# Reordering the early loads and bias adds of a 4096-cubed matmul with bias and tanh on one Trainium2 core

## Chip, cores and metric

One NeuronCore of one Trainium2 chip runs the kernel. The metric is the device time of one execution in microseconds (us); the span in a profile, from the first to the last instruction, is about 1.7 us shorter.

## The reference

```python
m, k, n = 4096, 4096, 4096          # a, b, bias: random normal float32
return np.tanh(np.matmul(a, b) + bias)
```

## The kernel before

The matmuls are fp16 with float32 sums in PSUM: 32 row tiles of A, 32 k-tiles, output columns in 4 blocks of 1024 (two matmuls of 512 columns each). For columns 0 to 1023 the first eight row tiles run as two groups of four, g0 and g1, a few k-tiles at a time, so that matmuls can start while A and B are still arriving. Half-finished sums are set aside in SBUF ("spill"), and fills are matmuls on zeros. The steady loop comes after that and is not touched by the change. All loads that cast to fp16 are issued by GpSimd, in one queue; the kernel has at most eight of them in flight, each new issue waiting for the landing eight places before it.

The opening, cut (the comments are mine):

```python
fill(WARM, NB)                          # 11 matmuls on zeros
for t, copy in enumerate((nc.scalar.copy, nc.vector.tensor_copy)):
    load_b_low(nc.sync, raw_b[:, ds(t, 1), :], 0, t, 1)     # float32, 512 KB
    copy(b_cur[0][:, t, :], raw_b[:, t, :])                 # rounded to fp16
...
for m in g0:
    load_nat(m)                         # A's row tiles, 256 KB read each, GpSimd
...                                     # identity matrix
load_b_next(); load_b_next()            # B's third and fourth k-tile, GpSimd
turn_nat(0, nc.vector.tensor_copy); fill(3, P)   # 4 transposes on TensorE, one copy
turn_nat(1, nc.scalar.copy);        row(0, 0, 2)
turn_nat(2, nc.vector.tensor_copy); row(1, 0, 2)
turn_nat(3, nc.scalar.copy);        row(2, 0, 2); row(3, 0, 2)
```

The later loads and the end of the first eight row tiles, cut:

```python
want_a("g0c", G, 0, G * Q, KS, KM - KS)          # A, k-tiles 8 to 15, row tiles of g0
for u in range(KS, KM, 2):
    want(lambda u=u: load_b_all(u, 2))           # B, k-tiles 8 to 15
...
want(lambda: load_bias(bias_bc, 0, nc.gpsimd))
for t in (KM, KM + 8): ...                       # A for g1 and B, k-tiles 16 to 31
...
for t in (KM, KM + 8):
    for i in range(G):
        turn(ats[G + i], ("g1", t), i * Q, t, 8)        # VectorE transposes
    for m in g1 if t == KM else g0:
        for j in range(J):
            add_bias(m, j)                              # VectorE
    across(ps, g1, t, min(t + 8, KT - TB), KS)          # TensorE
turn(ats[0], ("g0", 0), 0, KM, KT - KM)                 # the first long transpose
down(ps, g1, KT - TB, KT, end)                          # g1 finished: add, tanh, store
...
for m in g0:
    for j in range(J):
        ...                                             # 16 matmuls
        if m < G - 1 and j == 0:
            turn(ats[m + 1], ("g0", m + 1), 0, KM, KT - KM)   # m = 0: the second one
        end(ps, m, j)
```

## Time and profile before

| | before |
|---|---|
| time, median of 3 runs | 1781.81 us (1781.77 to 1782.02) |
| span of the profiled run | 1780.2 us |
| TensorE busy | 1774.4 us, 100% |
| first real matmul | 7.44 us |
| breaks in TensorE's work after that | 0.08 us at 28.7, 0.21 at 35.8, 0.24 at 77.5 |

The page lists engine shares and the chain that ended last; the timeline prints start, duration, engine, source line, operation, what is written from what, the count, and in brackets the idle time before it and what ended it. PE is TensorE's matmuls, PEld its weight loads, DVE VectorE, ACT ScalarE, POOL GpSimd; L138 is line 138 of kernel.py, the matmul helper. On VectorE, L100 is a transpose of A, L176 and L149 add a PSUM bank to a spilled sum (L149 the last time), L181 adds the bias. A landing, below, is a load's issue plus its time to landing.

### The profile page before, as it was taken

Reading aid. Unit: us, or ns where it says so; the run is one execution under the profiler, and the core shown is the slowest. Engines: PE = TensorE matmul, PEld = TensorE weight load, DVE = VectorE, ACT = ScalarE, POOL = GpSimd, SP = SyncE. Lnnn points to the kernel's source line nnn. Section 1 sums busy time; section 2 is a strip of 40 time slices with the busy share of each in tenths; the row PEclk is TensorE's granted clock in tenths of the full one; section 3 lists DMA queues with packets and bytes.
Section 4 is the critical chain, followed back from the end, with each engine's and each line's share of the span. In section 5 each row is a group of like instructions: output and inputs, shape, how many; then the busy total and the mean of one; then the engine's idle time right before and its main releaser. Section 6 shows DMA issues by size and latency. Waiting matters only on the chain.

```text
span 1780.2 us, 20854 instructions
## 1 busy us (share of the span) xinstructions
PE 1774.4 (100%) x8254; PEld 806.9 (45%) x8254; DVE 763.8 (43%) x680; ACT 173.2 (10%) x279; POOL 872.1 (49%) x1618
## 2 busy tenths in 40 slices
PE   9999999999999999999999999999999999999999
PEld 4444444444444444444444444444444444444444
DVE  3764353444344443444344443444344443444342
ACT  2011000000000000000000000000000000000001
POOL 7465566544466554444456554444544454444510
PEclk9999999999999999999999999999999999999999
DMA  9999999976999877767699987766776667766641
GB/s 186 203 189 178 168 166 169 140 124 109 165 165 173 148 115 115 119 114 121 113 177 165 170 137 115 119 115 109 129 117 120 107 114 115 120 114 109 116 77 42
DMA packets 281393, 238.94 MB, mean 134 GB/s; under 512 B 159056, under 2 KB 231760, under 8 KB 281296
## 3 DMA queue, kind: packets, MB, share of 16 engines
q0 software_dynamic: 243280, 167.88, 70.1%
q1 hardware_dynamic: 37728, 69.62, 11.0%
q8 instruction: 64, 1.05, 0.2%
q14 instruction: 33, 0.27, 0.0%
q10 hardware_dynamic: 288, 0.13, 0.0%
HBM read 337.64 MB, written 67.11 MB: 227 GB/s over the span
## 4 chain that ended last, share of the span: by engine, by line
PE 99%; DMA 0%; issue 0%; ACT 0%; POOL 0%; DVE 0%; DVEq 0%; POOLq 0%
PE ps L412 93%; PE ps L138 6%; DMA nat<-in_a_dram 0%; ACT o_sb L152 0%; PE tp L257 0%; POOL nat L246 0%; DVE o_sb L149 0%; DVEq L149 0%; POOLq L435 0%
## 5 line engine op out<-in xcount | busy, mean ns | idle before, releaser
L412 PE MATMUL ps<-b,at 128*128 128x512 f16 x7712 | 1657.8, 378 | 0.0
L90 POOL DMA_DIRECT2D an<-in_a_dram x1492 | 805.5, 547 | 796.6 <-DVE at L100 583.4
L412 PEld LDWEIGHTS <-at 128*128 128x128 f16 x7712 | 754.6, 98 | 903.3
L100 DVE STREAM_TRANSPOSE at<-an 128x512 f16<-128x512 f16 (+1 forms) x380 | 565.6, 1539 | 85.8 <-DMA an<-in_a_dram 85.8
L149 DVE TENSOR_TENSOR o_sb<-ps,bias_bc 128x512 f32<-128x512 f32 (+1 forms) x243 | 165.4, 683 | 897.7 <-PE ps L412 695.7
L152 ACT ACTIVATE o_sb<-o_sb 128x512 f32<-128x512 f32 (+1 forms) x243 | 151.8, 626 | 1499.1 <-DVE o_sb L149 1499.1
L73 POOL DMA_DIRECT2D b<-in_b_dram x104 | 56.2, 544 | 15.5 <-DMA an<-in_a_dram 8.4
L138 PE MATMUL ps<-b,atx 128*128 128x512 f16 x256 | 56.2, 379 | 0.0
L138 PE MATMUL ps<-b,at 128*128 128x512 f16 x256 | 55.7, 379 | 0.1
L138 PEld LDWEIGHTS <-at 128*128 128x128 f16 x256 | 25.0, 98 | 30.5 <-DVE spill L181 0.5
L138 PEld LDWEIGHTS <-atx 128*128 128x128 f16 x256 | 24.6, 98 | 30.1 <-DVE atx L100 0.9
L100 DVE STREAM_TRANSPOSE atx<-an 128x512 f16<-128x512 f16 (+2 forms) x12 | 16.3, 1399 | 13.0 <-DMA an<-in_a_dram 13.0
L69 POOL DMA_DIRECT2D b<-in_b_dram x12 | 7.8, 654 | 22.4 <-PE ps L412 22.3
L152 ACT ACTIVATE spill<-spill 128x512 f32<-128x512 f32 x16 | 9.9, 632 | 85.6 <-DVE spill L149 85.5
L149 DVE TENSOR_TENSOR spill<-ps,spill 128x512 f32<-128x512 f32 x16 | 10.4, 678 | 9.9 <-PE ps L138 9.9
L181 DVE TENSOR_TENSOR spill<-spill,bias_bc 128x512 f32<-128x512 f32 x16 | 9.7, 680 | 0.0
L173 ACT COPY spill<-ps 128x512 f32<-128x512 f32 x16 | 8.0, 623 | 12.9 <-PE ps L138 12.9
L228 PE MATMUL ps<-zeros 128*128 128x512 f16 (+1 forms) x14 | 4.7, 498 | 1.3 <-DVE zeros L221 1.3
L176 DVE TENSOR_TENSOR spill<-ps,spill 128x512 f32<-128x512 f32 x8 | 4.8, 670 | 0.0
L228 PEld LDWEIGHTS <-zeros 128*128 128x128 f16 x14 | 1.6, 130 | 3.7 <-issue 2.4
L239 DVE CAST b<-spill 128x1024 f16<-128x1024 f32 x1 | 0.8, 849 | 4.5 <-DMA spill<-in_b_dram 4.5
L246 POOL DMA_DIRECT2D nat<-in_a_dram x4 | 2.3, 587 | 0.8 <-POOLq L435 0.8
(14 smaller groups left out, 8.9 us busy)
## 6 DMA issues: line engine op xcount, KB each, us to landing
an<-in_a_dram POOLq DMA_DIRECT2D x480, 192.0 KB, 5.1
out_dram<-o_sb SPq DMA_DIRECT2D x239, 256.0 KB, 2.7
an<-in_a_dram POOLq DMA_DIRECT2D x960, 32.0 KB, 2.7
b<-in_b_dram POOLq DMA_DIRECT2D x94, 256.0 KB, 8.2
b<-in_b_dram POOLq DMA_DIRECT2D x6, 1024.0 KB, 13.5
an<-in_a_dram POOLq DMA_DIRECT2D x32, 128.0 KB, 5.6
out_dram<-spill SPq DMA_DIRECT2D x16, 256.0 KB, 5.9
an<-in_a_dram POOLq DMA_DIRECT2D x12, 256.0 KB, 8.2
```

The costliest lines, as they stand in the source:

```text
L69: queue.dma_start(out=dst, in_=src[:, ds(t0 % BL, nt), :])
L73: nc.gpsimd.dma_start(out=bt[t0 // TB][ds(q * QP, QP), ds(t0 % TB, nt), :], in_=src.rearrange("(t p) n -> p t n", p=QP),)
L90: nc.gpsimd.dma_start(out=an[ds(q * QP, QP), :, ds((t - t0) * QP, n * QP)], in_=src.rearrange("(mb p) k -> p mb k", p=QP),)
L100: nc.vector.transpose(at[:, ds(t, n), :].rearrange("P t (mb p) -> P mb t p", p=QP), an[:, ds(mb0, Q), ds((t - t0) * QP, n * QP)].rearrange ...
L138: nc.tensor.matmul(ps, at[:, t, :], bt[t // TB][:, t % TB, ts(j, NB)], start=start, stop=stop)
L149: nc.vector.tensor_tensor(out=o_sb[:, piece], in0=ps[:, piece], in1=addend[:, piece], op=mybir.AluOpType.add)
L152: nc.scalar.activation(o_sb[:, piece], o_sb[:, piece], mybir.ActivationFunctionType.Tanh)
L173: nc.scalar.copy(aside(m, j), ps)
L176: nc.vector.tensor_tensor(out=aside(m, j), in0=ps, in1=aside(m, j), op=mybir.AluOpType.add)
L181: nc.vector.tensor_tensor(out=aside(m, j), in0=aside(m, j), in1=bias_bc[:, ts(j, NB)], op=mybir.AluOpType.add)
L228: nc.tensor.matmul(ps[:, ds(0, w)], zeros[:, :P], zeros[:, :w], start=i == 0, stop=i == n - 1)
L412: nc.tensor.matmul(ps, at[:, t, :], b_cur[t // TB][:, t % TB, ds(c0, w)], start=t == 0, stop=t == KT - 1,)
```

## The change

Its intent: the first matmul should not wait for two float32 k-tiles of B on SyncE's queue. Only the first stays there, rounded by two engines at once. The second goes to GpSimd's queue behind two row tiles. Later loads are split so that what is needed first lands first, and the bias moves back.

```diff
-    WARM = 11
+    WARM = 9
...
-    for t, copy in enumerate((nc.scalar.copy, nc.vector.tensor_copy)):
-        load_b_low(nc.sync, raw_b[:, ds(t, 1), :], 0, t, 1)
-        copy(b_cur[0][:, t, :], raw_b[:, t, :])
+    load_b_low(nc.sync, raw_b[:, ds(0, 1), :], 0, 0, 1)
+    for j, copy in enumerate((nc.scalar.copy, nc.vector.tensor_copy)):
+        copy(b_cur[0][:, 0, ts(j, NB)], raw_b[:, 0, ts(j, NB)])
...
-        copy(ats[m][:, ds(0, BL), :], tp)
+        for t in range(0, BL, 2):
+            copy(ats[m][:, ds(t, 2), :], tp[:, ds(t, 2), :])
...
-    for m in g0:
-        load_nat(m)
+    load_nat(0)
+    load_nat(1)
+    load_b_next()
+    load_nat(2)
     ...                                  # identity matrix
+    load_nat(3)
...
-    want_a("g0c", G, 0, G * Q, KS, KM - KS)
-    for u in range(KS, KM, 2):
-        want(lambda u=u: load_b_all(u, 2))
+    for t in (KS, KS + 4):
+        want_a(("g0", t), G, 0, G * Q, t, 4)
+        for u in (t, t + 2):
+            want(lambda u=u: load_b_all(u, 2))
...
-        for u in range(t, t + 8, TB):
-            want(lambda u=u: load_b_all(u, TB))
+        for u in (t, t + 2):
+            want(lambda u=u: load_b_all(u, 2))
+        if t > KM:
+            want(lambda: load_bias(bias_bc, 0, nc.gpsimd))
+        want(lambda t=t: load_b_all(t + TB, TB))
...
-        for m in g1 if t == KM else g0:
-            for j in range(J):
-                add_bias(m, j)
         across(ps, g1, t, min(t + 8, KT - TB), KS)
+    for m in g1:
+        for j in range(J):
+            add_bias(m, j)
     turn(ats[0], ("g0", 0), 0, KM, KT - KM)
     down(ps, g1, KT - TB, KT, end)
+    for m in g0:
+        for j in range(J):
+            add_bias(m, j)
```

Left out: the matmul order of the first two row tiles (one k-tile each, then fills, then the second k-tile), VectorE's transposes of A's k-tiles 8 to 15, cut in halves like their loads, and a later bias row loaded in two pieces.

More of the change, by code (lines that the diff above doesn't have):

```diff
@@ L257, in turn_nat @@
             nc.tensor.transpose(tp[:, t, :], nats[m][:, :, t], ident)
-        copy(ats[m][:, ds(0, BL), :], tp)
-    nats, b_done = {}, [2]
-    for m in g0:
-        load_nat(m)
+        for t in range(0, BL, 2):
+            copy(ats[m][:, ds(t, 2), :], tp[:, ds(t, 2), :])
+    nats, b_done = {}, [1]
+    load_nat(0)
+    load_nat(1)
+    load_b_next()
+    load_nat(2)
     nc.gpsimd.affine_select(
@@ L279 @@
     turn_nat(1, nc.scalar.copy)
-    row(0, 0, 2)
+    row(0, 0, 1)
+    row(1, 0, 1)
+    fill(4, P)
+    row(0, 1, 1)
     turn_nat(2, nc.vector.tensor_copy)
-    row(1, 0, 2)
+    row(1, 1, 1)
+    fill(3, P)
     turn_nat(3, nc.scalar.copy)
@@ L300 @@
     bias_bc = biasp.tile([P, NCW], fp32, name="bias_bc")
-    want(lambda: load_bias(bias_bc, 0, nc.gpsimd))
     for t in (KM, KM + 8):
         want_a(("g1", t), G, 4 * P, G * Q, t, 8)
-        for u in range(t, t + 8, TB):
-            want(lambda u=u: load_b_all(u, TB))
+        for u in (t, t + 2):
[3 more added lines that the diff above has]
+        want(lambda t=t: load_b_all(t + TB, TB))
     for m in g0:
@@ L325 @@
     ps = {}
-    for m in g0:
-        turn(ats[m], "g0c", m * Q, KS, KM - KS)
+    for t in (KS, KS + 4):
+        for m in g0:
+            turn(ats[m], ("g0", t), m * Q, t, 4)
     one_by_one(ps, g0, BL, KS, BL)
@@ L343 @@
             turn(ats[G + i], ("g1", t), i * Q, t, 8)
-        for m in g1 if t == KM else g0:
-            for j in range(J):
-                add_bias(m, j)
         across(ps, g1, t, min(t + 8, KT - TB), KS)
+    for m in g1:
+        for j in range(J):
+            add_bias(m, j)
     turn(ats[0], ("g0", 0), 0, KM, KT - KM)
     down(ps, g1, KT - TB, KT, end)
+    for m in g0:
+        for j in range(J):
+            add_bias(m, j)
     ahead = 3
@@ L398 @@
             bias_next = biasp.tile([P, NCW], fp32, name="bias_bc")
-            load_bias(bias_next, (c + 1) * NCW, nc.sync)
+            for h in range(2 if c == 0 else 1):
+                w = NCW // (2 if c == 0 else 1)
+                load_bias(bias_next[:, ds(h * w, w)], (c + 1) * NCW + h * w, nc.sync)
         pump()
```

## The prediction

> **What bounds the kernel now.** I read the engine shares first, then the chain that ended last, then the first 120 us in order of time, because the diff touches only work issued there.
>
> The page's engine rows and its chain of work:
>
> ```profile
> span 1780.2 us, 20854 instructions
> PE 1774.4 (100%) x8254; PEld 806.9 (45%) x8254; DVE 763.8 (43%) x680; ACT 173.2 (10%) x279; POOL 872.1 (49%) x1618
> PE 99%; DMA 0%; issue 0%; ACT 0%; POOL 0%; DVE 0%; DVEq 0%; POOLq 0%
> ```
>
> TensorE sets the time. The merged chain in order of time shows what little is not matmul:
>
> ```profile
> 1.31 0.68 POOL nat L246
> 2.00 5.12 DMA nat<-in_a_dram
> ...
> 9.79 25.99 PE ps L138 x120
> 35.78 0.05 issue
> 35.82 41.60 PE ps L138 x192
> 77.42 0.08 issue
> 77.50 41.60 PE ps L138 x192
> 119.10 1654.20 PE ps L412 x7680
> ```
>
> 41.60/192 = 0.217 us a matmul in the opening, 1654.20/7680 = 0.215 later. A saving can only come from the lead-in (7.4 us to the first real matmul) and from three small breaks. Two stand here: 35.82 starts 0.21 us and 77.50 about 0.24 us beyond the usual step. A third, 0.08 us, is at 28.70, below. Against 1781.8 us, 2% is 35.6 us: out of reach both ways unless something goes badly wrong.
>
> The timeline of the opening, TensorE, VectorE and the loads:
>
> ```profile
> 1.26 4.33 PE L228 MATMUL ps<-zeros 128*128 128x512 f16 x11 [1.26 <-DVE zeros L221]
> ...
> 5.88 0.85 DVE L239 CAST b<-spill 128x1024 f16<-128x1024 f32 x1 [4.53 <-DMA spill<-in_b_dram]
> ...
> 6.51 0.41 PE L257 MATMUL tp<-ident,nat 128*128 128x128 f16 x4 [0.91 <-DMA nat<-in_a_dram]
> ...
> 7.44 1.04 PE L138 MATMUL ps<-b,atx 128*128 128x512 f16 x4
> ...
> 27.93 2.50 DVE L100 STREAM_TRANSPOSE atx<-an 128x512 f16<-128x512 f16 x4 [6.30 <-DMA an<-in_a_dram]
> ...
> 28.69 6.59 PEld L138 LDWEIGHTS <-atx 128*128 128x128 f16 x32 [0.41 <-DVE atx L100]
> ```
>
> The reader should see that from 6.5 us TensorE never rests, and that at 28.69 it waits for VectorE, which waited for a load of A that landed at 27.85 (issued 19.34, 8.5 us to landing). That load has no slack.
>
> VectorE where the first pass ends, and a bias pass it did earlier:
>
> ```profile
> 76.36 4.86 DVE L181 TENSOR_TENSOR spill<-spill,bias_bc 128x512 f32<-128x512 f32 x8
> 85.07 2.31 DVE L100 STREAM_TRANSPOSE atx<-an 128x2048 f16<-128x2048 f16 x1 [3.85 <-DMA an<-in_a_dram]
> 87.31 4.90 DVE L149 TENSOR_TENSOR spill<-ps,spill 128x512 f32<-128x512 f32 x8
> 92.12 2.30 DVE L100 STREAM_TRANSPOSE atx<-an 128x2048 f16<-128x2048 f16 x1
> ```
>
> From 85.07 to 94.42 VectorE is full; its second long transpose feeds the row tile that TensorE reaches at 91.31 + 32 x 0.217 = 98.24. Slack: 3.8 us.
>
> **What the Trainium skill says.** "DMA: Bandwidth & Descriptors", section "Issuing engines are not separate DMA queues": loads issued by any engine run on the same 16 DMA engines and interleave, so issuing elsewhere saves sequencer time, not bandwidth. The trace agrees: the opening reads about 400 KB of float32 per us, whether from SyncE's queue (409 GB/s in 4 to 5 us) or from GpSimd's, whose page rate of about 200 GB/s counts the halved written bytes. "TensorE: Matmul & The Clock Gate", section "Part 1: The HAM clock gate": the clock is released after some 3.4 us of activity, not after a number of matmuls. The trace agrees: fills step by 0.427 us from 1.26 to about 4.9, then go twice as fast. The same page, section "Architectural detail", says VectorE's queue is strictly first in, first out. At 87.31 above it agrees: finished sums wait behind the 85.07 transpose, which waits for its load.
>
> **The change, part by part.**
>
> Lead-in. Before, both of B's first k-tiles (512 KB each, SyncE) precede A's row tiles (256 KB each read). Landings, issue plus time to landing: B0 4.6, B1 5.9, row tiles 6.5, 7.1, 7.8, 8.4, then B2 9.7, B3 10.9. That is 0.65 us per 256 KB. Now GpSimd's queue holds row 0, row 1, B1, row 2, row 3, B2, B3; the bytes are the same. Placing each landing by the KB before it: row 0 after 768 KB, two steps earlier, 5.2; row 1 5.8; B1 7.1; row 2, row 3, B2, B3 unchanged. Eleven fills less two at 0.427 cold, the last two already fast, end near 5.1, about when row 0 lands.
> B0 rounded in halves by ScalarE and VectorE costs some 0.5 us instead of ScalarE's 1.05, ready by about 5.2. First real matmul: row 0 lands at 5.2; before, landing to matmul took 7.44 - 6.46 = 1.0 us; so about 6.1, 1.3 us earlier. But row 2 lands at 7.8 and row 3 at 8.4 still. Row 3's four transposes then start near 8.65 (9.19 before), row 2's matmuls near 8.9 (9.6 before). So the lead is 0.7 us once all four rows run. The added fills, 7 x 0.06 = 0.4 us, mostly lie in waits for B1 and row 3.
>
> The lead then dies. TensorE would reach the 28.70 point at about 28.0, but its data land at 27.85 because loads up to there have the same order and bytes, and the DMA engines are busy. Ready at 28.64 as before. Worth: 0, or the 0.08.
>
> A's k-tiles 8 to 15 in two halves with B's between. B8 and B9, which ended the wait at 35.8 (landing 35.73: 28.13 + 7.6), now come after 4 small A loads instead of 4 large. Small ones land about 0.73 us apart, large ones 1.33. So 27.85 + 4 x 0.73 + 4 x 0.64 = 33.3, needed at 35.6: 0.21 us saved. Price: 8 x 0.73 - 4 x 1.33 = about 0.4 us more queue time for all later loads.
>
> B24 and B25 as two k-tiles with bias later: about 73.4 instead of 77.3, and 24 through 27 by 76.0, so the 0.24 us at 77.50 goes too. Together 0.45 us saved; TensorE ends the first group's last stage at about 90.9.
>
> Bias adds moved. Two passes of eight adds, 4.86 us each, ran at 61.05 and 76.36, when VectorE was otherwise waiting for loads. The first now runs at about 77.8 to 82.6, still free. The second now stands behind the last finished sums and ahead of the second long transpose, and there is no slack for it. Chain from the load that frees 85.07:
> - first long transpose: 85.07 to 87.31 (next start)
> - eight finished sums, spaced 0.6: to 92.1
> - eight bias adds, spaced 0.6: to 96.9
> - second long transpose, 2.30: to 99.2.
>
> TensorE wanted it at 98.24 before, at 97.8 now. So it waits some 1.4 us and restarts 0.95 us later than before; with the 0.4 us that the load behind the first transpose lost, 1.35 us later. After that VectorE catches up (5 us of work per 6.9 us row tile). The next A row's buffer is released 5 us later, but it landed at 109.4 for a transpose at 112.8, so I expect no second wait. From 119 to the end all is matmul and shifts as a block. The bias row in two pieces later costs nothing visible.
>
> Sum: lead-in 0, breaks -0.45, new wait about +1.8 = **+1.35 us: 1781.8 + 1.3 = 1783.1 us**.
>
> **The rivals.**
> First, the change works as intended: the loads of A for 28.70 come 0.7 us or more sooner because two queues fill the DMA ramp at 2 to 4 us better. For it: only 193 GB/s flow in 2 to 3 us, and in 16 to 18 us the rate sags below what such packets reach elsewhere, so there is room. Against it: the loads between wait for earlier landings (GpSimd has eight in flight), and B3, whose landing releases them, moves only if the total does. If the DMA stream gains 1 us throughout, the late chain starts 1 us earlier too: about 1782.0. If it gains 2 us, 1781.2.
> Second, GpSimd's first load may have a start-up of its own. Its first packet appears at 4.85 us, 3.5 us after issue, where later isolated issues take about 1.25. I read this as waiting behind SyncE's megabyte. If it is start-up instead, the DMA engines idle from about 3.9 to 4.8 and everything slips up to 0.9 us: 1784.0.
> Third, the bias adds slip into gaps: no wait at 98, total 1781.4. VectorE's order in the program speaks against it: the eight adds precede the transpose.
>
> **Range and chances.** All terms together move the time by under 3 us. I take **1783.1 us**, 8 in 10 within **1781.2 to 1784.3**. Chances: **faster by over 2% 0.003, within 2% 0.994, slower by over 2% 0.003**.
>
> **What would show it.** In the changed profile: first real matmul near 6.1; TensorE's loads at about 28.7 still waiting for VectorE, with a break near 0.7 us; no break at 35.8 or 77.5; L181-type adds at about 92 to 97 and, right behind, a weight load near 99 that waited over 1 us for the long transpose. The prediction is wrong if that weight load does not wait, or if the 28.7 break is absent because the loads came earlier, or if a new break appears before 20 us.

## More of the kernel before

In the records each load raises its semaphore in 16 steps, which I read as one per DMA engine. I call the time from first to last step the load's *spread*; it is worked out from the trace's semaphore records.

## The result and the profile after

| | before | after |
|---|---|---|
| time, median | 1781.91 us (4 runs, 1781.77 to 1782.03) | 1785.53 us (4 runs, 1784.90 to 1786.65) |
| ratio of the fast runs | | 1.0021, 95% interval 1.0004 to 1.0038 |
| span of the profiled run | 1780.2 us | 1784.9 us |

A ratio is the mean time of one kernel's fast runs over that of the other's in the same rounds, so it is not quite the ratio of the medians. The changed kernel is slower by 0.2%, inside the 2% band, but 3.6 us by the medians where I had 1.3, and outside my range. The profiled run is the slowest of its four; a second profile follows below.

The page's engine row and chain row after the change:

```profile
span 1784.9 us, 20891 instructions
PE 1774.9 (99%) x8259; PEld 805.9 (45%) x8259; DVE 763.7 (43%) x686; ACT 172.5 (10%) x281; POOL 876.2 (49%) x1631
PE 94%; DMA 3%; POOL 1%; issue 1%; DVE 1%; ACT 0%; DVEq 0%; POOLq 0%
```

TensorE's busy time is the same to 0.5 us, so what was added is waiting. The chain now leaves TensorE for 6% of the span: it runs through loads and VectorE up to 102.84 us and is pure matmul from there on.

The timeline of the opening after the change, TensorE alone:

```profile
5.20 0.41 PE L257 MATMUL tp<-ident,nat 128*128 128x128 f16 x4 [0.28 <-DMA nat<-in_a_dram]
...
6.80 0.41 PE L257 MATMUL tp<-ident,nat 128*128 128x128 f16 x4 [1.03 <-DMA nat<-in_a_dram]
...
7.05 1.23 PE L138 MATMUL ps<-b,atx 128*128 128x512 f16 x4
```

The first row tile arrives as early as intended: its transposes start at 5.20 instead of 6.51. The second is 1 us late, and TensorE idles for it.

Waits of TensorE from 20 to 54 us, after the change, from its timeline:

```profile
23.16 7.12 PE L138 MATMUL ps<-b,at 128*128 128x512 f16 x32 [0.54 <-DMA b<-in_b_dram]
30.78 20.89 PE L138 MATMUL ps<-b,atx 128*128 128x512 f16 x96 [0.50 <-DVE atx L100]
52.63 1.67 PE L138 MATMUL ps<-b,at 128*128 128x512 f16 x7 [0.95 <-DVE spill L176]
```

Two are for late loads, directly or through VectorE's transposes of them. The third waits for VectorE to empty a PSUM bank; VectorE had stood behind transposes whose load was late (49.51, before 46.08). The bracket subtracts part of the pipelined matmul; by start-to-start times less the usual 0.217 the three cost 0.71, 0.67 and 1.12 us. The breaks at 35.8 and 77.5 are gone.

VectorE after the change, around the end of group g1, and the weight load that waits for it:

```profile
81.75 4.91 DVE L181 TENSOR_TENSOR spill<-spill,bias_bc 128x512 f32<-128x512 f32 x8 [3.16 <-DMA bias_bc<-in_bias_dram]
88.67 2.31 DVE L100 STREAM_TRANSPOSE atx<-an 128x2048 f16<-128x2048 f16 x1 [2.02 <-DMA an<-in_a_dram]
90.91 4.84 DVE L149 TENSOR_TENSOR spill<-ps,spill 128x512 f32<-128x512 f32 x8
95.67 4.89 DVE L181 TENSOR_TENSOR spill<-spill,bias_bc 128x512 f32<-128x512 f32 x8
100.47 2.31 DVE L100 STREAM_TRANSPOSE atx<-an 128x2048 f16<-128x2048 f16 x1
```

```profile
102.83 1.19 PEld L138 LDWEIGHTS <-atx 128*128 128x128 f16 x7 [2.19 <-DVE atx L100]
```

This is the chain I had drawn: transpose, eight finished sums, eight bias adds, transpose, and TensorE waiting behind. From the start of the first transpose to TensorE's restart it takes 102.84 - 88.67 = 14.17 us. I had 85.07 to 99.2, 14.1 us. What is different is where it starts: its load landed at 88.55, before at 84.88, in my estimate at about 85.3.

How late is the same matmul in the two traces, counted from the first real one? 0.39 us early at the first, 0.74 late at the 9th, 2.08 at the 101st, 2.99 at the 201st, 2.75 at the 416th, 4.62 at the 417th (the one at 102.84), and 4.63 at the 8001st. The last wait makes 1.87 us, the loads before it 2.75.

Landings, us, by the trace's records:

| load | before | my estimate | after |
|---|---|---|---|
| A's row tile 1 | 6.46 | 5.2 | 5.15 |
| A's row tile 2 | 7.11 | 5.8 | 6.76 |
| B's second k-tile | 5.86 | 7.1 | 8.60 |
| A's row tile 3 | 7.80 | 7.8 | 9.25 |
| A's row tile 4 | 8.41 | 8.4 | 9.91 |
| B's third k-tile | 9.67 | 9.7 | 11.75 |
| B's fourth k-tile | 10.93 | 10.9 | 13.11 |
| the load of A that frees the 28.7 point | 27.85 | 27.85 | 29.82 |
| the load before the first long transpose | 84.88 | 85.3 | 88.55 |

From row tile 2 on, loads are late although the bytes are the same. Busy time by stretch, the kernel before and then the changed one (columns: stretch and its length; busy us and count of TensorE, its weight loads, VectorE, ScalarE, GpSimd; clock; DMA share; GB/s written):

```profile
7.00:8.00 1.00, 0.93 (x9) 0.57 (x8) 0.38 (x1) 0.39 (x1) 0.91 (x2) 1.00 1.28 215
8.00:9.00 1.00, 1.00 (x10) 0.56 (x8) 0.26 (x1) 0.20 (x1) 0.88 (x2) 1.00 1.09 204
9.00:10.00 1.00, 1.00 (x9) 0.60 (x8) 0.16 (x1) 0.17 (x1) 0.32 (x2) 1.00 1.13 211
```

```profile
7.00:8.00 1.00, 0.97 (x8) 0.36 (x7) 0.00 (x0) 0.65 (x2) 0.58 (x1) 1.00 1.18 179
8.00:9.00 1.00, 0.87 (x8) 0.37 (x6) 0.00 (x0) 0.00 (x0) 0.12 (x1) 1.00 1.21 172
9.00:10.00 1.00, 0.94 (x9) 0.47 (x8) 0.25 (x2) 0.00 (x0) 0.92 (x2) 1.00 1.05 175
```

The DMA engines were as busy but wrote 175 GB/s for 210. The semaphore records say in which form: before, the spread of the opening's loads was 0.6 us; after, row tile 2 spread 1.46 us, B's second k-tile 1.81, the fourth 2.00. A load counts as landed only with its slowest engine.

The spread is how the slip begins, not how it lasts. Once there it stays between 1.76 and 2.03 us from B's second k-tile to the load that lands at 15.28, with no new step at each load, and is 0.57 again at the load that lands at 16.01. What passes the slip on is the limit of eight loads in flight: the issue that waits for B's fourth k-tile to land left at 11.21 us before and at 13.40 after, and from 13 to 17 us the engines wrote 101 and 104 GB/s (each for 2 us) where they had written 128 and 143. At the 28.7 load the spreads are alike (1.90 before, 1.82 after), and its first step is as late as its last (2.06 and 1.97 us).

### The profile page after: what moved, and what is told of

The parts are those of the page before. It is cut to its first block, busy times and chain, and to the rows that moved or that the text cites. A ratio compares the mean times of both kernels' runs of the same rounds, so it can differ in the third digit from the quotient of the medians.

```text
span 1784.9 us, 20891 instructions
## 1 busy us (share of the span) xinstructions
PE 1774.9 (99%) x8259; PEld 805.9 (45%) x8259; DVE 763.7 (43%) x686; ACT 172.5 (10%) x281; POOL 876.2 (49%) x1631
## 4 chain that ended last, share of the span: by engine, by line
PE 94%; DMA 3%; POOL 1%; issue 1%; DVE 1%; ACT 0%; DVEq 0%; POOLq 0%
PE ps L429 93%; DMA an<-in_a_dram 2%; DMA b<-in_b_dram 1%; PE ps L138 1%; POOL an L90 1%; DMA bias_bc<-in_bias_dram 0%; DVE spill L181 0%; DVE spill L149 0%; POOL b L73 0%; DVE atx L100 0%; POOL b L69 0%; POOL nat L246 0%; ACT o_sb L152 0%; DVE o_sb L149 0%; POOL ident L266 0%
## 5 line engine op out<-in xcount | busy, mean ns | idle before, releaser
L73 POOL DMA_DIRECT2D b<-in_b_dram x112 | 60.2, 541 | 12.2 <-DMA an<-in_a_dram 7.0
L100 DVE STREAM_TRANSPOSE atx<-an 128x512 f16<-128x512 f16 (+1 forms) x16 | 16.7, 1086 | 13.8 <-DMA an<-in_a_dram 13.8
L69 POOL DMA_DIRECT2D b<-in_b_dram x13 | 8.4, 651 | 16.1 <-PE ps L429 15.8
L228 PE MATMUL ps<-zeros 128*128 128x128 f16 (+1 forms) x19 | 4.7, 393 | 1.3 <-DVE zeros L221 1.3
```

The costliest lines, as they stand in the source:

```text
L69: queue.dma_start(out=dst, in_=src[:, ds(t0 % BL, nt), :])
L73: nc.gpsimd.dma_start(out=bt[t0 // TB][ds(q * QP, QP), ds(t0 % TB, nt), :], in_=src.rearrange("(t p) n -> p t n", p=QP),)
L100: nc.vector.transpose(at[:, ds(t, n), :].rearrange("P t (mb p) -> P mb t p", p=QP), an[:, ds(mb0, Q), ds((t - t0) * QP, n * QP)].rearrange ...
L228: nc.tensor.matmul(ps[:, ds(0, w)], zeros[:, :P], zeros[:, :w], start=i == 0, stop=i == n - 1)
```

## The experiments

Theory A: the second block of eight bias adds turns the late load behind the first long transpose into TensorE time. Theory C: the new opening makes the loads slip. Rival D: the finer later loads make the loss, the opening is harmless. Fifteen runs in three batches of four and one of three; kernels of one batch share a chip and its runs of the kernel before. The scatter was wider than in the first comparison: the kernel before ran 1781.59 to 1782.80 in the first batch (median 1782.20), 1781.52 to 1783.19 in the second (1781.76) and 1781.72 to 1784.21 in the third and fourth (1782.38).

**e1_adds_in_loop**: each bias add stands just ahead of the finished sum that needs it.

```diff
     down(ps, g1, KT - TB, KT, end)
-    for m in g0:
-        for j in range(J):
-            add_bias(m, j)
...
                 new_at(j)
+            add_bias(m, j)
             end(ps, m, j)
```

> The changed kernel with one move: the second pass of eight bias adds is no longer in one block after the first group's last stage, each add stands just ahead of the finished sum that needs it. Theory A (the block of adds delays the second long transpose, which TensorE awaits at 102.8): the 1.9 us wait near 100 us goes away, and the time falls by 1.7 to 2.0 us, to about 1783.7; the three earlier waits (23.2, 30.8, 52.6) stay. Rival B (the late loads alone set that point, the adds lie in the wait for them): no more than 0.5 us.

1783.72 us (1782.67 to 1784.97), ratio to before 1.0009 (0.9997 to 1.0022), against 1.0021 for the whole change. VectorE and the weight loads in its timeline:

```profile
89.95 4.84 DVE L149 TENSOR_TENSOR spill<-ps,spill 128x512 f32<-128x512 f32 x8
94.72 2.29 DVE L100 STREAM_TRANSPOSE atx<-an 128x2048 f16<-128x2048 f16 x1
96.93 0.65 DVE L181 TENSOR_TENSOR spill<-spill,bias_bc 128x512 f32<-128x512 f32 x1
```

```profile
97.07 7.00 PEld L138 LDWEIGHTS <-atx 128*128 128x128 f16 x33
```

The transpose follows the finished sums directly, and no weight load waits, although the load behind the first transpose was late here too (87.60). Its matmuls are 1.66 us late: three waits at 22.3, 30.1 and 51.5 that the loads cause (2.19 us), less the three old breaks (0.53). The median fell as theory A says. The two ratios' intervals overlap, so it is the missing wait in the trace that shows the cause.

**e2_opening_only**: the kernel before with only the opening of the changed one (the first four parts of the diff and the matmul order).

> The kernel before with the opening of the changed kernel alone (nine fills, B's second k-tile on GpSimd's queue behind two row tiles, halves in rounding and copying, the row order); everything after it as before. Theory C (the opening makes the loads slip: B's fourth k-tile landed at 13.1 us and not at 10.9, and the slip stays in a full queue): B's fourth k-tile lands 1.5 to 2.5 us late, waits near 23 and 31 us, the time rises by 1.5 to 2.5 us to about 1784. Rival D (the later splitting of A and B loads makes the loss, the opening is harmless or gains): within 0.5 us of before, and the first landings as I predicted (7.1, 7.8, 8.4, 9.7, 10.9).

1782.93 us (1782.47 to 1784.05), ratio 1.0006 (0.9993 to 1.0018). B's fourth k-tile landed at 12.12, 1.19 late; row tile 2's spread was 1.23. TensorE waits at 29.5 for a load 0.74 late, and at 78.7. So the slip of theory C is real, but in this run half of what the changed kernel showed, and it costs about 0.7 us by the medians rather than 1.5 to 2.5. The interval of the ratio includes 1; in the trace, later matmuls are 1.25 us late.

**e3_rest_only**: the changed kernel with the old opening.

> The changed kernel with the old opening: only the later parts of the change are in. Theory C with A: the old landings come back (B's fourth k-tile at 10.9), no waits at 23, 30.8 (over 0.1), 35.8 or 77.5; TensorE waits 1.3 to 1.5 us near 98 for the second long transpose; the time is what I predicted for the whole change, 1783.1 (plus or minus 0.4). Rival D: 1785 or more.

1785.20 us (1783.74 to 1789.47), ratio 1.0020 (1.0006 to 1.0034): as slow as the whole change, against theory C's number and as rival D's has it. VectorE and the weight load:

```profile
87.22 2.31 DVE L100 STREAM_TRANSPOSE atx<-an 128x2048 f16<-128x2048 f16 x1 [2.10 <-DMA an<-in_a_dram]
...
94.22 4.88 DVE L181 TENSOR_TENSOR spill<-spill,bias_bc 128x512 f32<-128x512 f32 x8
99.02 2.30 DVE L100 STREAM_TRANSPOSE atx<-an 128x2048 f16<-128x2048 f16 x1
```

```profile
101.38 2.70 PEld L138 LDWEIGHTS <-atx 128*128 128x128 f16 x14 [3.32 <-DVE atx L100]
```

The opening's landings are back (B's fourth k-tile 10.99, the 28.7 load 27.81), and its 416th matmul is only 0.17 us late. Yet the load behind the first transpose landed at 87.10, 2.2 us later than before and 1.8 later than I had it. TensorE had slack for that; the block of adds took the slack away. One wait of 3.0 us makes nearly the whole loss of 3.2 in this trace. Rival D is right that the later parts alone can cost this much; that the opening is harmless is refuted by e2's landings.

**e4_b1_on_sync**: the changed kernel, B's second k-tile back on SyncE's queue.

```diff
-    load_b_low(nc.sync, raw_b[:, ds(0, 1), :], 0, 0, 1)
-    for j, copy in enumerate((nc.scalar.copy, nc.vector.tensor_copy)):
-        copy(b_cur[0][:, 0, ts(j, NB)], raw_b[:, 0, ts(j, NB)])
+    for t in range(2):
+        load_b_low(nc.sync, raw_b[:, ds(t, 1), :], 0, t, 1)
+        for j, copy in enumerate((nc.scalar.copy, nc.vector.tensor_copy)):
+            copy(b_cur[0][:, t, ts(j, NB)], raw_b[:, t, ts(j, NB)])
...
-    load_b_next()                        # between row tiles 2 and 3
```

> The changed kernel with B's second k-tile back on SyncE's queue right behind the first, all else of the change kept (fills, halves, row order of the matmuls, later loads). Theory E (it is the second k-tile on GpSimd's queue between the row tiles that spreads the 16 DMA engines' finishing times from 0.6 to 1.5 us and more): the spread is 0.6 to 0.8 again, B's fourth k-tile lands at 10.9 plus or minus 0.3, the time is 1783.1 plus or minus 0.5. Rival F (the slip comes from the copies in halves or from TensorE and VectorE work at other times, or is luck of the run): B's fourth k-tile still lands at 12 or later, time above 1784.5.

The landings did what theory E said: spreads 0.41 to 0.61 in the opening, B's fourth k-tile at 11.13. The time did not: 1785.86 us (1784.29 to 1786.61), ratio 1.0020 (1.0007 to 1.0032). Its profile is of its fastest run: wait 1.49 us at 100.1, the load at 85.85.

**e5_rest_adds_in_loop**: e3 with the adds spread out as in e1.

> The old opening with the later parts of the change, and the second pass of bias adds taken out of its block, each add ahead of its finished sum. Theory A (the block turned every late landing of the load behind the first long transpose into TensorE time: 3.2 us in the run with the block): no wait near 100 us, the time falls by about 3 us against that run, to 1782.2 plus or minus 0.5. Rival (the later loads cost time elsewhere): above 1784.

1783.17 us (1782.28 to 1783.29), ratio 1.0006 (0.9992 to 1.0019), where e3 had 1.0020. The load was as late as in e3 (86.91), and TensorE did not wait near 100 at all. By the ratios the adds' place is worth about 0.0014 x 1782 = 2.5 us, but the two intervals make that uncertain by 0.0019 (3.4 us); it is the trace that shows it, as 3.0 us of wait that is gone. The time stayed 0.5 us above what was expected at most: waits of 0.4 and 0.7 us remain at 29.3 and 50.7.

**e6_splits_only**: the kernel before with the finer loads of A and B only (and the later bias row in two pieces).

> The kernel before with only the loads of A and B split finer (A's k-tiles 8 to 15 in two halves with B between, B's k-tiles in pairs); opening, bias load and bias adds as before. Prediction's own term: the waits at 35.8 and 77.5 go, 0.45 us saved. Rival, after the runs so far (the finer A loads hold the queue up and bring a wait near 50 us, where the bank-freeing adds stand behind a transpose whose load is late): waits at 35.8 and 77.5 gone, one of 0.4 to 1.0 us at 50, the time within 0.5 us of before, none of it gained.

1783.11 us (1782.00 to 1784.28), ratio 1.0007 (0.9994 to 1.0019). VectorE around 50 us:

```profile
47.72 2.37 DVE L100 STREAM_TRANSPOSE at<-an 128x1024 f16<-128x1024 f16 x2 [6.36 <-DMA an<-in_a_dram]
50.02 4.83 DVE L176 TENSOR_TENSOR spill<-ps,spill 128x512 f32<-128x512 f32 x8
```

The breaks at 35.8 and 77.5 are gone, and a wait of 1.07 us at 50.7 has taken their place, because the adds that free PSUM banks stand behind transposes of a load that is 1.5 us late. The rival's structure held; the wait was just above its upper bound, and the time above its half microsecond.

**e7_b1_behind_rows**: the kernel before, only B's first k-tile on SyncE's queue, the second behind all four row tiles.

> The kernel before with B's second k-tile on GpSimd's queue behind all four row tiles, first k-tile rounded by two engines. Theory G (a B tile between row tiles spreads the DMA engines): every spread of the first eight loads, first engine done to last, is 0.4 to 0.8 us, the row tiles land at about 5.1, 5.8, 6.5, 7.1. Rival H (the cause is the short SyncE queue: a single k-tile there and the casting loads starting sooner): the second row tile's spread is 1.2 us or more as in the three runs with the new opening.

1785.57 us. Spreads 1.31, 1.30, 0.95 and 1.30 for the four row tiles, with no B tile between them, which refutes theory G and fits rival H. TensorE then stood still for B's second k-tile (landed 10.27), and its clock fell back; see the last section.

**e8_b1_uncast**: e2 with B's second k-tile at its new place, but loaded as float32 and rounded by ScalarE and VectorE.

> The new opening on the old rest, B's second k-tile at its new place on GpSimd's queue but loaded as float32 and rounded by ScalarE and VectorE. Theory G': it is the casting of the tile that spreads the engines: the spread of row tile 2 is back to 0.4 to 0.8 us, the tile lands at about 7.1. Rival H (queue position or start time, not the cast): spread 1.2 us or more again.

1782.78 us. Row tile 2 spread 1.53 us, the k-tile landed at 8.41. The cast of this tile is not the cause.

**e9_sync_twice**: e2 with a second 512 KB load on SyncE's queue that nobody reads.

```diff
-    load_b_low(nc.sync, raw_b[:, ds(0, 1), :], 0, 0, 1)
+    for t in range(2):
+        load_b_low(nc.sync, raw_b[:, ds(t, 1), :], 0, t, 1)
```

> The new opening on the old rest, and SyncE's queue carries a second 512 KB load that nobody reads, so that GpSimd's loads begin to flow at about 4.9 us as in the kernel before, while B's second k-tile stays on GpSimd's queue between the row tiles. Theory J (the engines spread because GpSimd's loads flow from 3.6 us on, while GpSimd is still issuing): spreads of the row tiles 0.4 to 0.8 us; landings about 6.5, 7.1, B's second 8.4. Rival K (the order of loads on GpSimd's queue spreads them): row tile 2 or B's second k-tile 1.2 us or more.

1783.14 us. With the same order on GpSimd's queue, row tiles 1 to 4 spread 0.60, 0.60, 0.60 and 0.72, B's second k-tile 0.61. So the order in the queue is not the cause; SyncE's second load ahead of the flow, or the later start that it brings, undoes the spread.

**e10_gpsimd_pause**: e2, but GpSimd waits for row tile 1 to land before it issues anything after row tile 2.

```diff
     load_nat(1)
+    nc.gpsimd.affine_select(...)         # moved up
+    pause = singles.tile([P, 1], fp16, name="pause")
+    nc.gpsimd.tensor_copy(pause, nats[0][:, 0, ds(0, 1)])
     load_b_next()
```

> The new opening on the old rest, but after the second row tile GpSimd waits until the first has landed (about 5.2 us) before it issues more. Theory J, in its form that GpSimd's issuing beside flowing loads is what spreads the engines: row tile 2 now flows with nothing being issued and its spread falls to 0.8 us or less. Rival L (the early start of the flow alone, or the end of SyncE's load): 1.2 us or more again. The time will be worse, as all later loads are held back.

1785.58 us. Row tile 2 spread 0.90: between the two bounds, so undecided.

**e11_after_again**: the changed kernel once more.

> The changed kernel once more, for a second profile. By theory A the restart after the wait near 100 us is the landing of the load behind the first long transpose plus 14.3 us, whatever that landing is; the last wait is 1 to 3 us; time 1784.5 to 1786.5.

1785.60 us (1785.22 to 1788.13), ratio 1.0020 (1.0007 to 1.0033). In this profile the load landed at 87.50 and TensorE restarted at 101.79: 14.29 us later, as in the first profile (88.55 and 102.84). e3 has 101.38 - 87.10 = 14.28, e4 100.13 - 85.85 = 14.28. The wait was 1.33 us.

**e12_late_pair_only**: the kernel before with only B's k-tiles 24 to 27 in pairs.

> The kernel before with one part of the change that I still count as a gain: B's k-tiles 24 to 27 loaded in pairs, so that the first pair lands 2.5 us sooner. The break of 0.24 us at 77.5 goes, nothing else moves: 1781.5, that is 0.2 us under before; less than the runs' own scatter, so the trace decides. Rival: the queue's slips move the landing more than that and the time stays within 0.5 us on either side.

1782.19 us (1781.82 to 1782.30), ratio 0.9997 (0.9984 to 1.0011). The break at 77.5 is gone from the trace, and its span is 1780.1, the one before 1780.2. The times do not tell it from the kernel before; it is not shown to beat it.

**e9b_sync_twice, e10b_gpsimd_pause, e10c_gpsimd_pause**: e9 once and e10 twice more, for the open question of the spread.

> The kernel with the second, unread SyncE load again. Theory J (an early start of GpSimd's flow spreads the engines): row tiles and B's second k-tile spread 0.5 to 0.8 us again. Rival K (the order on GpSimd's queue): 1.2 us or more.

> The kernel with GpSimd's pause again. Theory J in the form of issuing beside the flow: row tile 2 spreads 0.8 us or less. Rival L (the early start alone): 1.2 us or more.

> The same kernel with GpSimd's pause a third time, with the same two expectations: 0.8 us or less for issuing beside the flow, 1.2 us or more for the early start alone.

e9b: 1783.16 us, spreads 0.60 to 0.69. e10b: 1784.87 us, row tile 2 spread 0.53; e10c: 1785.36 us, 0.65. Both fall under the bound of 0.8 that the issuing form of theory J sets. But what follows does not fit it. GpSimd issued without a break from 5.34 to 11.80 us in e10b and from 5.17 to 11.35 in e10c, and B's second k-tile and row tiles 3 and 4, which landed from 9.24 to 10.94 beside that issuing, spread only 0.47 to 0.85. The wide spread comes back with B's third k-tile, at 13 us: 1.35 and 1.44. In the kernel before, too, GpSimd issued until 6.21 us while row tile 1 flowed, with a spread of 0.62. So issuing beside the flow is not enough to spread the engines. The pause also left nothing queued behind row tile 2, a rival that no run separates.

The runs side by side (us). "Opening": n new, o old, 2 new with an unread second SyncE load. "A finer": A's k-tiles 8 to 15 in halves. "Late load" is the landing before the first long transpose; "wait" is TensorE's wait near 100 us.

| run | opening | A finer | block of adds | spread of row tile 2 | B's fourth | 28.7 load | B's k-tile 15 | late load | wait |
|---|---|---|---|---|---|---|---|---|---|
| before | o | no | no | 0.59 | 10.93 | 27.85 | 43.37 | 84.88 | 0 |
| after | n | yes | yes | 1.46 | 13.11 | 29.82 | 46.78 | 88.55 | 1.87 |
| e11 | n | yes | yes | 1.46 | 12.76 | 29.62 | 46.57 | 87.50 | 1.33 |
| e1 | n | yes | no | 1.34 | 11.91 | 29.09 | 45.69 | 87.60 | 0 |
| e2 | n | no | no | 1.23 | 12.12 | 28.59 | 44.16 | 86.24 | 0 |
| e8 | n | no | no | 1.53 | 12.32 | 28.28 | 43.88 | 85.77 | 0 |
| e9b | 2 | no | no | 0.64 | 12.34 | 28.85 | 44.63 | 86.21 | 0 |
| e3 | o | yes | yes | 0.43 | 10.99 | 27.81 | 44.09 | 87.10 | 2.99 |
| e4 | o | yes | yes | 0.47 | 11.13 | 27.71 | 44.47 | 85.85 | 1.49 |
| e5 | o | yes | no | 0.80 | 11.30 | 28.42 | 44.51 | 86.91 | 0 |
| e6 | o | yes | no | 0.72 | 11.16 | 27.70 | 44.87 | 85.54 | 0 |
| e12 | o | no | no | 0.54 | 11.11 | 27.86 | 43.97 | 85.23 | 0 |

e4 keeps the new copies and matmul order, but its loads are those of the old opening; e9b reads 512 KB more.

## Why the prediction was wrong

**The late chain: right.** Eight adds ahead of the second long transpose, with no slack, was the mechanism I named. Its length came out as 14.3 us from landing to restart in four profiles, where my steps give 99.2 - 84.88 = 14.3. Taking the block out (e1 against the change, e5 against e3) took the wait out. The third rival, adds slipping into gaps, is refuted by each of the four waits. That the wait itself, 1.87 us, met my "about +1.8" is luck: the chain started 3.27 us later than I had it, and TensorE, 2.75 us late where I had it 0.45 early, came 3.20 us later to wait for it.

**The failed step: where the chain starts.** I let it start 0.4 us late, from one term, the smaller A loads. In the first profile it started 3.67 us late (88.55 for 84.88), in the second 2.62. That is the term that was mis-sized, and it closes the sum: my 1.35 plus the missing 3.27 is 4.62, the lateness measured at the restart; in the second profile 1.35 plus 2.22 is 3.57, and 3.57 was measured. The lateness of the load has three parts.

First, "the bytes are the same" and so "row 2, row 3, B2, B3 unchanged", with the lead-in at 0. With the new opening and no unread load the 28.7 load landed at 29.82, 29.62, 29.09, 28.59 and 28.28 (mean 29.08); with the old one at 27.85, 27.81, 27.71, 28.42, 27.70 and 27.86 (27.89). So the opening costs some 1.2 us of queue (e7 and the pause runs have other openings and are left out). I had counted bytes at one rate and not asked whether all 16 engines would stay together. The experiments narrow the cause: it is not the place of B's tile between the row tiles (e7), nor its cast (e8), each in one look. What differs is that GpSimd's loads flow from 3.6 us on instead of 4.85. Delaying the flow behind SyncE restored the spread of the row tiles to 0.6 (e9, e9b); so did, in two runs of three, a pause of GpSimd with the early start kept (0.53, 0.65 and once 0.90). So neither the early start nor GpSimd's issuing does it alone, and why an engine falls behind stays open.

Second, the price of the finer A loads, for which I had 0.4 us (my own figures, 8 x 0.73 - 4 x 1.33, give 0.52). From the 28.7 load to B's k-tile 15 it is 15.5 to 16.1 us in the ten runs without them, and in those with them 16.96, 16.95, 16.60, 16.28, 16.76, 16.09 and 17.17: about 0.9 us more than the mean of the ten. The saving of 0.45 us at 35.8 and 77.5 was right to the digit, but e6 shows it given back at 50 us, a wait that I had not looked for.

Third, a rest of about 0.5 us between k-tile 15 and the late load (41.9 us on average in the six runs with the bias late, 41.4 in the other eleven). The two sets overlap, so this part stays open.

**The lead: partly right, then lost.** Row tile 1 at 5.15 was my 5.2. The first real matmul came at 7.05 where I had 6.1, because row(0) stands behind the transposes of row tile 2, which landed at 6.76 and not 5.8. The lead of 0.7 us that I expected after row tile 4 was a lag of 0.74. That a lead would die at 28.7 could then not be seen. The break there, 0.67 us where I had about 0.7, is a second number met by luck: data and TensorE were both some 2 us later than I had them. One of my signs of being wrong did come: a new break before 20 us. From the first real matmul to the ninth TensorE went from 0.39 us early to 0.74 late.

**The rivals.** The first, a faster DMA ramp, did not occur: 2 to 3 us moved 156 GB/s, before 193. The second, a start-up of GpSimd's first load, is refuted by row tile 1's landing at 5.15. Its direction, a slip of up to 0.9 us, was the right one, for another reason; I gave it too little room, and my range ended at 1784.3.

**How the parts combine.** TensorE's loss is not a sum of parts. In e3 the late load cost nothing until the block of adds exposed it; in e1 the same lateness was mostly slack. By the ratios the opening alone (1.0006) and the rest alone (1.0020) add up to 1.0026 where the whole has 1.0021; with intervals of 0.0012 to 0.0017 to each side, they do not tell whether the parts add.

## What to carry to other kernels

Before moving work on an in-order engine, write down the landing that starts its chain and how far that landing itself can slip; a chain without slack passes on every slip, whatever caused it. Equal bytes do not mean equal landings: a load ends with its slowest DMA engine, so compare the first and last of a load's semaphore steps, and follow which later issue waits for that last step. When a break is removed, look for the next instruction on the same engine that had its slack from it.

## What the Trainium skill lacked or had wrong

- The Trainium skill's page "DMA: Bandwidth & Descriptors", section "Issuing engines are not separate DMA queues", says that the issuing engine only saves issue time. No page that I read says that an earlier start of GpSimd's loads can change how evenly the 16 engines finish: at row tile 2 it is 0.4 to 0.8 us from first to last in the eight runs with SyncE's megabyte ahead, 1.2 to 1.5 us in the five runs e1, e2, e8, e11 and after without it, and 175 GB/s written instead of 210 in 9 to 10 us.
- The same page, section "Latency and other measured facts", offers contention at the rings of GpSimd's descriptors as a best guess for two slower engines. One late engine fits row tile 2 of the changed kernel, whose last step came 0.58 us after the last but one (6.18, 6.76), but the trace does not name engines, and before, with the same kind of load, that gap was 0.13 us. Not shown either way.
- "Runtime: NRT & Kernel Launch", section "Instruction fetch mechanics", says that 16 KiB blocks of instructions are fetched by DMA, mostly hidden. The trace of the kernel before shows packets of 16384 bytes near 21, 47, 75 and 100 us, each of which takes 0.94 to 0.98 us of a DMA engine (up to 1.78 in other runs). The load that landed next after the third, at 77.26, came 1.78 us after the load ahead of it instead of 1.25. That a fetch holds up ordinary loads is my reading; no run isolated it.
- "TensorE: Matmul & The Clock Gate", section "Part 1: The HAM clock gate", puts the fall to half rate after about 3.4 us idle. In e7 a pause of 3.0 us and in e10 one of 2.06 us was followed by matmul steps of 0.427 us; in e10b one of 1.98 us was not. The clock records of these runs change in steps of 3.41 us (e10: up at 6.46, down at 9.87, up at 13.28). TensorE stood idle for 2.88 and 1.90 us of the 3.41 us that ended in the fall in e7 and e10, and for 1.54 us of the stretch that held most of the pause in e10b. So in e10 a stretch that was a little over half idle was enough. As far as these three runs tell, it is where the pause falls among the stretches that parts e10 from e10b.
